# A state-space layer's decay product, made whole or in two halves of a block's tokens

## The chip, the cores and the metric

One core of one Trainium2 chip runs the whole program. The time is the device time of one execution in microseconds (us). A profile gives, for one execution, the start and length of every instruction on the core's engines: TensorE (PE, with its weight loads listed apart as PEld), VectorE (DVE), ScalarE (ACT), GpSimd (POOL) and SyncE (SP), which here issues the transfers.

## The reference

A trunk of two layers over 256 tokens of width 2048. The first layer is a Mamba-2 mixer (SSD): a projection to z, x, B, C and dt, a causal convolution, a state-space scan, a gate and a grouped RMS norm, and a projection back. The second is a dilated attention with shared keys and values. Both are followed by a residual and a LayerNorm. The part that matters here is the scan, cut from the reference; the sequence is one chunk of 256 tokens, so the state that comes in is zero and y is y_diag:

```python
G, K, P, N = 8, 8, 64, 128        # groups, heads per group, head width, state
acum  = jnp.cumsum(ac, axis=1)                        # log decays, per token and head
seg   = acum[:, :, None] - acum[:, None, :]           # from token s to token l
decay = jnp.exp(jnp.where(causal, seg, -jnp.inf))
cb    = jnp.einsum("blgn,bsgn->blsg", cc, bc)         # C_l . B_s, per group
y_diag = jnp.einsum("blsgk,bsgkp->blgkp", cb[..., None] * decay, xc)
...
y = y + (xs * D_skip[:, None]).reshape(bsz, L, SSD_D_INNER)
y = y * jax.nn.silu(z)
```

For each of 64 heads this is the product of a lower triangular matrix of 256 x 256 (C.B times the decay) with the head's 256 x 64 columns of x times dt.

## The kernel before

All large products are made with weights split into two rounded parts (`hi` and `lo`, lines 92 to 98), in three matmuls for each pair of tiles: lines 121 to 123 (channels in the partitions), 169 to 171 (tokens in the partitions), and 145 and 148 in the second layer. Their weights are streamed from memory in pieces of 512 KB (line 89), split by ScalarE (line 95) and VectorE (line 97). These products fill nearly all of TensorE's time from the first layer to the end.

The scan runs group by group, eight heads in each. Each group has three stages:

- `stage1(g)` (line 548) makes C.B for three blocks of 128 x 128 tokens (lines 554 and 555; source and target both in the first 128 tokens, both in the second, and from the first to the second), the two diagonal blocks of the decay of every head on ScalarE (lines 567 and 569), their product `seg` (line 570), and by transposes (line 578) the columns `xd`, which are x times dt.
- `stage2(g)` (line 595) makes the part that comes from the first block to the second (line 600, one product for all eight heads of the group, the decay being split off), and then, for each of the two blocks `b` of 128 tokens, eight products into one PSUM tile `py` of 128 x 512: one for each head, with the head's 128 x 128 matrix `seg` as stationary operand and its 64 columns of `xd` as moving operand (line 608). VectorE adds `py` to y (line 609) and multiplies by the gate (line 610); ScalarE squares it and sums (line 611).
- `stage3(g)` (line 616) applies the norm's factor.

All operands of line 608 are f32; the profile records each such product as two passes, that is two weight loads and two matmuls.

The order of the work is that of the program's lines as the framework's scheduler places them on each engine: between `stage1(g)` and `stage2(g)` stands the projection `product("z", g + 1)`, so that TensorE has products of the next group while ScalarE makes the decays. TensorE executes in the placed order. Around line 608's blocks stand line 600 ahead and the projections' products (lines 121 to 123 and 169 to 171) behind; the last group's blocks are interleaved with the last projection's products. Two more lines appear in the prediction for their shapes: 461, transposes of dt with 64 rows in use, and 544 and 258, transposes with 64 and 16 columns.

The PSUM tiles `py` come from the pool `aux2`, with two buffers, so the next block's products don't wait for VectorE to have read the last one.

Of the kernel before, what the change touches and what calls it, by code (L numbers as in the profile page):

```python
# [49 lines left out]
def trunk(ctx, tc, xT, x, c, par, cst, bias, lnrow, ada, wdt, win, wout, wk, wv, wbin, wbout, out):  # L50
    nc = tc.nc
    V, S, T, PO = nc.vector, nc.scalar, nc.tensor, nc.gpsimd
# [148 lines left out]
    def rsqrt(v, tag):  # L201

        y = sm.tile(list(v.shape), F32, name=tag + "y")
        sh = sm.tile(list(v.shape), I32, name=tag + "s")
        V.tensor_scalar(sh, v.bitcast(I32), 1, None, op0=ALU.logical_shift_right)
        V.tensor_tensor(y.bitcast(I32), magic[:, :v.shape[1]], sh, op=ALU.subtract)
        t = sm.tile(list(v.shape), F32, name=tag + "t")
        for _ in range(3):
            V.tensor_tensor(t, y, y, op=ALU.mult)
            V.scalar_tensor_tensor(t, t, -0.5, v, op0=ALU.mult, op1=ALU.mult)  # L210
            V.scalar_tensor_tensor(y, t, 1.5, y, op0=ALU.add, op1=ALU.mult)
        return y
# [73 lines left out]
    with ExitStack() as cA:  # L286
# [14 lines left out]
        with ExitStack() as cS:  # L301
# [293 lines left out]
            def stage2(g, segs, xd, cb, xo):  # L595

                ss = sm.tile([P, 2], F32, name="ss")

                po = aux.tile([P, 512], F32, name="aux")
                T.matmul(po, cb[:, 2, :], xo, start=True, stop=True)  # L600
                V.tensor_tensor(xo.rearrange("p (h e) -> p h e", h=HPG), po.rearrange("p (h e) -> p h e", h=HPG),
                                dec[:, 1, g * HPG:(g + 1) * HPG, None].to_broadcast([P, HPG, 64]), op=ALU.mult)
                V.tensor_tensor(y[g][:, 1, :], xo, y[g][:, 1, :], op=ALU.add)
                for b in range(2):
                    py = aux2.tile([P, 512], F32, name="py")
                    for hh in range(HPG):
                        e_ = slice(64 * hh, 64 * hh + 64)
                        T.matmul(py[:, e_], segs[hh // 4][:, hh % 4, b, :], xd[:, b, e_], start=True, stop=True)  # L608
                    V.tensor_tensor(y[g][:, b, :], py, y[g][:, b, :], op=ALU.add)
                    V.tensor_tensor(y[g][:, b, :], y[g][:, b, :], sz[g][:, b, :], op=ALU.mult)  # L610
                    S.activation(py, y[g][:, b, :], AF.Square, accum_out=ss[:, b:b + 1])
                ms = sm.tile([P, 2], F32, name="ms")
                V.tensor_scalar(ms, ss, 1.0 / 512, EPS, op0=ALU.mult, op1=ALU.add)
                return rsqrt(ms, "a")
# [8 lines left out]
            for g in range(G - 1):  # L623
                if g == 1:
                    pin[0] = latest[-1].ins
                    queue(wp1, [(0, "gate", kt) for kt in range(KT)])
                    jobs.append(lambda: gate_out(0))
                if g % 2 == 1:
                    product("bc", g + 1)
                product("xs", g + 1)  # L630
                if rs is not None:
                    stage3(g - 1, rs)
                st1 = stage1(g)
                if g < G - 2:
                    product("z", g + 1)
                rs = stage2(g, *st1)
# [7 lines left out]
            product("z", G - 1, last_scores)  # L644
            drain()
            stage3(G - 1, stage2(G - 1, *st1))
        aux = ctx.enter_context(tc.tile_pool(name="auxb", bufs=2, space=PSUM, reuse_waits="tile"))

# [428 lines left out]
```

## Time and profile before

| | |
|---|---|
| median of 3 runs | 1275.34 us (1275.26 to 1276.29) |
| span of the profiled execution, first to last instruction | 1272.5 us |
| median less that span (the profiled execution's own whole time isn't listed apart) | 2.8 us |
| instructions | 19056 |
| TensorE busy, matmuls / weight loads | 1236.6 us / 1078.7 us |
| VectorE / ScalarE busy | 1034.5 us / 704.0 us |
| read from memory | 332.47 MB, 263 GB/s over the span |

A line of a group of instructions reads: source line, engine, operation, written tile <- read tiles, for TensorE the rows*columns of the array that it uses, shape out, count | busy us in all, ns of one | idle time of the engine just before them, and what ended it. A line of the timeline reads: start, length, engine, source line, operation, and xN where N like it follow one another. Matmuls are pipelined: their records overlap, so the distance from one to the next, not the length of one, is what a pass takes. In the chain, each piece is the time that counts towards the end.

### The profile page before, as it was taken

How to read it: one execution, taken by the hardware profiler on the slowest of the kernel's cores; microseconds unless marked ns; L12 is line 12 of the kernel's file. 1: busy time of each engine (PE TensorE's matmuls, PEld its weight loads, DVE VectorE, ACT ScalarE, POOL GpSimd, SP SyncE). 2: the span in 40 equal slices, each digit the busy share in tenths (PEclk: the TensorE clock that was granted, in tenths of full speed). 3: DMA queues.
4: the chain of work that ended last, by engine and by line, in shares of the span. 5: the costliest groups of instructions: out<-in, count | busy, mean ns of one | idle time of the engine just before them, and what ended most of it. 6: DMA issues, size and time to landing. Idle time of an engine off the chain costs nothing.

```text
span 1272.5 us, 19056 instructions
## 1 busy us (share of the span) xinstructions
PE 1236.6 (97%) x7222; PEld 1078.7 (85%) x7222; DVE 1034.5 (81%) x1498; ACT 704.0 (55%) x1035; POOL 0.2 (0%) x4
## 2 busy tenths in 40 slices
PE   4999999999999999999999999999999999999997
PEld 4889989899898999778888788888878888888885
DVE  6999986999998878869776678878888867758876
ACT  3655577757677777764344445434345645444731
POOL 0000000000000000000000000000000000000000
PEclk9999999999999999999999999999999999999999
DMA  9999968696866546468988469989998774463751
GB/s 386 423 420 422 420 211 298 224 341 234 314 247 208 157 149 216 167 216 292 338 282 282 160 195 353 357 328 348 357 381 316 235 240 130 127 204 100 222 192 66
DMA packets 80588, 335.89 MB, mean 264 GB/s; under 512 B 9105, under 2 KB 9329, under 8 KB 67697
## 3 DMA queue, kind: packets, MB, share of 16 engines
q1 hardware_dynamic: 80496, 334.69, 73.5%
q8 instruction: 56, 0.92, 0.3%
q14 instruction: 36, 0.29, 0.1%
HBM read 332.47 MB, written 2.18 MB: 263 GB/s over the span
## 4 chain that ended last, share of the span: by engine, by line
PE 85%; DVE 8%; DMA 3%; issue 2%; ACT 1%; SPq 0%; DVEq 0%; ACTq 0%
PE acc L145 14%; PE acc L171 12%; PE acc L170 12%; PE acc L169 12%; PE acc L148 7%; PE acc L123 7%; PE acc L121 7%; PE acc L122 7%; DVE araw L247 2%; DVE wlo L97 2%; PE py L608 2%; PE aux L850 1%; DMA araw<-in_ada 1%; DMA raw<-in_wk 1%; PE po L873 1%
## 5 line engine op out<-in xcount | busy, mean ns | idle before, releaser
L95 ACT ACTIVATE whi<-raw 128x1024 fp32r<-128x1024 f32 x392 | 411.3, 1058 | 369.4 <-PE acc L171 127.3
L97 DVE TENSOR_TENSOR wlo<-raw,whi 128x1024 fp32r<-128x1024 f32 x392 | 473.3, 1220 | 140.3 <-ACT whi L95 139.5
L145 PE MATMUL acc<-actT,whi 128*128 128x512 f32 x896 | 285.9, 398 | 0.0
L170 PE MATMUL acc<-wlo,actT 128*128 128x512 f32 x688 | 269.7, 392 | 1.1 <-DVE wlo L97 0.9
L169 PE MATMUL acc<-whi,actT 128*128 128x512 f32 x688 | 266.7, 394 | 0.9 <-ACT actT L663 0.9
L121 PE MATMUL acc<-actT,whi 128*128 128x256 f32 x768 | 217.4, 285 | 17.5 <-ACT actT L398 17.3
L247 DVE SCALAR_TENSOR_TENSOR araw<-araw,cb__72 128x2048 f32<-128x2048 f32 x96 | 219.2, 2284 | 14.6 <-DMA araw<-in_ada 14.5
L123 PE MATMUL acc<-actT,wlo 128*128 128x256 f32 x768 | 214.9, 285 | 4.9 <-DVE wlo L97 4.9
L122 PE MATMUL acc<-actT,whi 128*128 128x256 f32 x768 | 217.1, 284 | 0.0
L148 PEld LDWEIGHTS acc<-actT,wlo 128*128 128x128 f32 x896 | 167.0, 188 | 42.1 <-DVE wlo L97 5.0
L148 PE MATMUL acc<-actT,wlo 128*128 128x256 f32 x896 | 180.9, 282 | 1.9 <-DVE wlo L97 1.2
L171 PE MATMUL acc<-whi,actT 128*128 128x512 f32 x432 | 168.7, 391 | 0.0
L121 PEld LDWEIGHTS acc<-actT,whi 128*128 128x128 f32 x768 | 147.7, 193 | 18.7 <-ACT actT L398 17.5
L170 PEld LDWEIGHTS acc<-wlo,actT 128*128 128x128 f32 x688 | 129.3, 188 | 29.1 <-DVE wlo L97 3.4
L123 PEld LDWEIGHTS acc<-actT,wlo 128*128 128x128 f32 x768 | 146.5, 193 | 6.0 <-DVE wlo L97 5.8
L169 PEld LDWEIGHTS acc<-whi,actT 128*128 128x128 f32 x688 | 128.7, 188 | 26.7 <-ACT actT L663 1.4
L122 PEld LDWEIGHTS acc<-actT,whi 128*128 128x128 f32 x768 | 148.1, 193 | 0.3
L145 PEld LDWEIGHTS acc<-actT,whi 128*128 128x128 f32 x896 | 137.5, 189 | 0.3
L171 PE MATMUL acc<-whi,ylo 128*128 128x512 f32 x256 | 100.5, 393 | 0.0
L171 PEld LDWEIGHTS acc<-whi,actT 128*128 128x128 f32 x432 | 81.1, 188 | 16.6
L171 PEld LDWEIGHTS acc<-whi,ylo 128*128 128x128 f32 x256 | 48.0, 188 | 9.7
L319 DVE SCALAR_TENSOR_TENSOR cacc<-acc,prm,cacc 128x253 f32<-128x253 f32 (+2 forms) x96 | 42.1, 474 | 6.1 <-ACT cacc L316 5.8
(251 smaller groups left out, 1110.2 us busy)
## 6 DMA issues: line engine op xcount, KB each, us to landing
araw<-in_ada SPq DMA_DIRECT2D x96, 1024.0 KB, 7.5
raw<-in_win SPq DMA_DIRECT2D x160, 512.0 KB, 5.6
raw<-in_wout SPq DMA_DIRECT2D x64, 512.0 KB, 4.8
raw<-in_wbin SPq DMA_DIRECT2D x64, 512.0 KB, 4.3
raw<-in_wv SPq DMA_DIRECT2D x48, 512.0 KB, 5.4
raw<-in_wk SPq DMA_DIRECT2D x48, 512.0 KB, 7.7
cbc<-cumd SPq DMA_DIRECT2D x16, 512.0 KB, 5.2
raw<-in_wbout SPq DMA_DIRECT2D x16, 512.0 KB, 4.7
```

Source lines behind the costliest of these rows:

```text
L95: copied.append(S.activation(hi, raw, AF.Copy))
L97: latest.append(V.tensor_tensor(lo, raw, hi.bitcast(F32), op=ALU.subtract))
L121: T.matmul(o, hi[:, k, c_], ahi[:, kt, :], start=first, stop=False, skip_group_check=True)
L122: T.matmul(o, hi[:, k, c_], alo[:, kt, :], start=False, stop=False, skip_group_check=True)
L123: T.matmul(o, lo[:, k, c_], ahi[:, kt, :], start=False, stop=kt == k1 - 1, skip_group_check=True)
L145: T.matmul(ps[n], hi[:, k, n * P:n * P + P], xp[:, kt], start=kt == 0, stop=False, skip_group_check=True)
L148: T.matmul(ps[n][:, 0, :], lo[:, k, n * P:n * P + P], xhi[:, kt, :], start=False, stop=kt == KT - 1, skip_group_check=True)
L169: T.matmul(o, h_, hi[:, k, :], start=kt == k0, stop=False, skip_group_check=part)
L170: T.matmul(o, h_, lo[:, k, :], start=False, stop=False, skip_group_check=part)
L171: end = T.matmul(o, l_, hi[:, k, :], start=False, stop=kt == k1 - 1, skip_group_check=part)
L247: V.scalar_tensor_tensor(raw, raw, 1.0, cb_, op0=ALU.mult, op1=ALU.mult, accum_out=mod[layer][:, ct, j:j + 1])
L319: V.scalar_tensor_tensor(acc[:, o:], ps[:, :L - o], w[:, j:j + 1], acc[:, o:], op0=ALU.mult, op1=ALU.add)
```

## The change

Each head's product with a block's 128 tokens is issued as two: one with the first 64 columns of the stationary matrix, which are the first 64 of the block's tokens, into partitions 0 to 63 of `py`, and one with the other 64 columns into partitions 64 to 127. Both read the same 64 moving columns. The sum over the 128 source tokens, the results and what follows stay as they are.

```diff
                     for hh in range(HPG):
                         e_ = slice(64 * hh, 64 * hh + 64)
-                        T.matmul(py[:, e_], segs[hh // 4][:, hh % 4, b, :], xd[:, b, e_], start=True, stop=True)
+                        for t_ in (slice(0, 64), slice(64, 128)):
+                            T.matmul(py[t_, e_], segs[hh // 4][:, hh % 4, b, t_], xd[:, b, e_], start=True, stop=True)
                     V.tensor_tensor(y[g][:, b, :], py, y[g][:, b, :], op=ALU.add)
```

## The prediction

> **What bounds the kernel now.** I read the page's busy times and its chain first, then the chain in order of time for the places where the changed line stands, then that line's own groups, and last the timeline of TensorE (PE) and of its weight loads (PEld) around one of its blocks.
>
> ```profile
> PE 1236.6 (97%) x7222; PEld 1078.7 (85%) x7222; DVE 1034.5 (81%) x1498; ACT 704.0 (55%) x1035; POOL 0.2 (0%) x4
> ...
> PE 85%; DVE 8%; DMA 3%; issue 2%; ACT 1%; SPq 0%; DVEq 0%; ACTq 0%
> ```
>
> TensorE is busy for 97% of the span and carries 85% of the chain that ends last. In the stage that the change touches it is no different; the row below is that of the 310 us in which all products of line 608 lie. Its first numbers are the length of the stretch and PE's busy time.
>
> ```profile
> 225.00:535.00 310.00, 306.22 (x2154) 284.12 (x2152) 278.56 (x449) 228.54 (x375) 0.00 (x0) 1.00 0.65 225
> ```
>
> PE leaves 3.8 us of 310 idle, at a granted clock of 1.00. So what PE needs more or less for line 608 is nearly all time of the kernel, as far as those products are on the chain. Which are, the chain in order of time tells (start, length, what):
>
> ```profile
> 229.24 1.73 PE py L608 x16
> ...
> 232.00 1.73 PE py L608 x16
> ...
> 287.85 3.52 PE py L608 x32
> ...
> 338.63 3.52 PE py L608 x32
> ...
> 382.63 3.52 PE py L608 x32
> ...
> 429.36 3.52 PE py L608 x32
> ...
> 502.48 3.52 PE py L608 x32
> ...
> 525.16 0.61 PE py L608 x6
> 533.58 1.08 PE py L608 x10
> ```
>
> The line's source view says how many there are in all, and the timeline of PE shows the three runs that the chain lacks:
>
> ```profile
> L608 PEld LDWEIGHTS py<-xd,seg x256: 186/192/192, 228.9 to 534.3; 128*128 128x128 f32 x128
> L608 PE MATMUL py<-xd,seg x256: 217/275/275, 229.1 to 534.4; 128*128 128x64 f32 x128
> ```
>
> ```profile
> 472.36 3.68 PE L608 MATMUL py<-xd,seg 128*128 128x64 f32 x32
> ...
> 518.43 1.02 PE L608 MATMUL py<-xd,seg 128*128 128x64 f32 x8
> ...
> 520.71 1.00 PE L608 MATMUL py<-xd,seg 128*128 128x64 f32 x8
> ```
>
> Each of the 128 f32 products is recorded as two passes, each a weight load and a matmul: 256 passes. They lie in 12 unbroken runs. Nine of these, with 16+16+5x32+6+10 = 208 passes (0.81 of all), are on the chain; at 472 and 518 VectorE is later, and PE has some time to spare.
>
> **What one pass costs, and what sets it.** The weight loads of one run, then the matmuls:
>
> ```profile
> 287.26 0.19 PEld L608 LDWEIGHTS py<-xd,seg 128*128 128x128 f32 x1 [0.24 <-issue]
> 287.69 3.54 PEld L608 LDWEIGHTS py<-xd,seg 128*128 128x128 f32 x31 [0.24 <-issue]
> ```
>
> ```profile
> 286.83 1.02 PE L600 MATMUL aux<-xo,cb 128*128 128x512 f32 x2
> 287.69 3.68 PE L608 MATMUL py<-xd,seg 128*128 128x64 f32 x32
> ```
>
> ```profile
> L600 PE MATMUL aux<-xo,cb 128*128 128x512 f32 x16 | 8.2, 594 | 0.0
> ```
>
> 31 loads of 0.192 us start within 3.54 us, so they follow each other by (3.54 - 0.19)/30 = 111.6 ns. The moving side would be quicker: the two passes of L600 are 1.02 - 0.59 = 0.43 us apart (0.59 is the mean of one, by its row of the groups) for 512 columns, 0.84 ns a column, or 54 ns for 64 columns. So a pass of line 608 is bound by loading 128 stationary columns, not by streaming 64. All of it now: 256 x 111.6 ns = 28.6 us.
>
> **The change part by part.** It makes 256 products of 64 stationary columns out of 128 of 128 columns, so 512 passes. Operands, values, the sums into py, the waits of line 609 on it, and every DMA stay; no step is moved and no wait is added. Only PE gets 256 more loads and 256 more matmuls.
>
> *A load of 64 columns.* No row has a plain f32 load of 64 columns. Other groups show how a load shrinks with its columns:
>
> ```profile
> L608 PEld LDWEIGHTS py<-xd,seg 128*128 128x128 f32 x256 | 30.4, 192 | 4.3 <-issue 3.3 <-DVE xd L580 0.5 <-DVE s L583 0.2
> L578 PEld LDWEIGHTS aux<-cc,xs 128*128 128x128 f32 x64 | 7.5, 141 | 1.7 <-DVE cb L557 1.1
> L544 PEld LDWEIGHTS aux<-cc,cumT 128*64 128x64 f32 x2 | 0.2, 110 | 0.2
> ...
> L258 PEld LDWEIGHTS aux<-cc,mod 128*16 128x16 f32 x2 | 0.2, 93 | 0.0
> ```
>
> The last three are transposes, which load faster: 141, 110 and 93 ns for 128, 64 and 16 columns, about 0.4 ns a column over a fixed 87 ns. Line 608's plain load takes 192, so (192 - 87)/128 = 0.82 ns a column: 105 ns of the 111.6 are columns and 6.6 are overhead. With 64 columns I estimate 52.5 + 6.6 = 59 ns a pass, just above the 54 ns of streaming. 512 x 59 = 30.2 us against 28.6: **+1.6 us**. The nearest row from above is line 461, the only one with 64 moving columns and a load of about this streaming length (transposes of a 64-row tile):
>
> ```profile
> 173.40 0.19 PEld L169 LDWEIGHTS acc<-whi,actT 128*128 128x128 f32 x1
> 173.94 0.20 PEld L461 LDWEIGHTS acc<-cc,dtrow 64*128 64x128 f32 x2 [0.35 <-ACT dtrow L458]
> 174.21 0.19 PEld L170 LDWEIGHTS acc<-wlo,actT 128*128 128x128 f32 x1
> ```
>
> ```profile
> 173.39 0.39 PE L171 MATMUL acc<-whi,actT 128*128 128x512 f32 x1
> 173.62 0.39 PE L169 MATMUL acc<-whi,actT 128*128 128x512 f32 x1
> 173.94 0.34 PE L461 MATMUL acc<-cc,dtrow 64*128 64x64 f32 x2
> 174.21 0.50 PE L170 MATMUL acc<-wlo,actT 128*128 128x512 f32 x1
> ```
>
> Its two loads (141 ns each, from its neighbour L578) span 0.20 us, so they are 0.06 us apart. At 63 ns the term is 512 x 63 - 28.6 = +3.7 us; at the streaming bound of 54 ns, -1.0 us. I take 59, whose slope comes from the load itself.
>
> *Going into and out of halves of the array.* The same rows price a change of tile. Elsewhere a load starts with the matmul ahead of it (173.40 and 173.39). Behind line 461's 64-row tile it doesn't: the second matmul started at about 173.94 + 0.34 - 0.22 = 174.06 (0.22 being the shortest matmul of 64 columns in line 608's row), and the next load, full size, only at 174.21: **0.15 us** later than in the usual order, and the matmul with it. The entry can't be read there, since that load waited for ScalarE (0.35 us). Behind line 258, which has only 16 columns but all rows, there is no such gap, the load comes with the matmul:
>
> ```profile
> 973.10 0.09 PEld L258 LDWEIGHTS aux<-cc,mod 128*16 128x16 f32 x1
> 973.32 0.30 PEld L169 LDWEIGHTS acc<-whi,actT 128*128 128x128 f32 x2
> ```
>
> ```profile
> 973.32 0.27 PE L258 MATMUL aux<-cc,mod 128*16 128x128 f32 x1
> 973.35 0.71 PE L169 MATMUL acc<-whi,actT 128*128 128x512 f32 x2
> ```
>
> So a switch costs between nothing and 0.15 us. I take 0.15, and as much for an entry, since the change, unlike line 258, places products in a part of the array that doesn't begin at its edge (PSUM's partitions from 64 on). 12 runs, 2 x 0.15 each: +3.6 us; for the nine runs on the chain 2.7.
>
> The Trainium skill, "TensorEngine Tiling (Array Packing)", section "Tiling Modes", says that changing the tiling mode, as opposed to the tile, drains TensorE. By it entry and exit both cost, and the two halves inside a run, being of one mode, don't: that is the 3.6 us; by the row alone, which shows an exit, it would be 1.8 us. The row agrees with the rule as far as it goes, for a 64-row tile and not for a 64-column one.
>
> *Sum.* On the chain: 0.81 x 1.6 + 2.7 = 1.3 + 2.7 = **+4.0 us**; with nothing absorbed at 472 and 518, +5.2. The span is 1272.5 us; the runs' median is 1275.34, 2.8 us around it, which I leave as it is: 1275.3 + 4.0 = **1279.3 us**. Behind py nothing else gets late first: in PE's order the products of the next group's columns follow, which have their weights, and the VectorE sum of line 609 starts later by what a run got longer, up to 0.1 + 0.15 us.
>
> **The rivals.**
>
> *The two halves load side by side (faster).* If a load into the second half of the array runs while the first half still loads, two passes take the time of one: 256 x 59 = 15.1 us, -13.5 us on the columns, +3.6 on switches: -9.9 if all of it counts, 0.81 x -13.5 + 2.7 = -8.2 on the chain: 1265.4 to **1267.1 us**. It decides from 28.6 - 3.6 = 25.0 us for 512 passes, under 49 ns each. Against it: in the rows above a load starts no earlier than the matmul ahead of it (287.26 is the start of L600's second pass, 286.83 + 0.43), and the change issues two passes into the same half in a row. For it: no product of this trace alternates between two halves, so no row excludes it. The Trainium skill's same section states that tiles operate independently and that different tiles can execute loads and matmuls in parallel; by that rule the time is this rival's. Chance 0.27.
>
> *Passes can't follow each other faster than about 110 ns (much slower).* No run of more than two passes in this trace is quicker than line 608's or the transposes' (about 109 ns). If instruction supply, or a load that can't hide beside a matmul in a half array (53 + 54 + 6 ns), holds a pass at 107 to 113 ns, or a 64-column load takes as long as a whole one, the columns cost 512 x 107 to 113 - 28.6 = 26 to 29 us; the spare time at 472 and 518 is used up by that, and with the switches it is +30 to +33: **1305 to 1308 us**. Against it: line 461's two passes in 0.06 us, and loads that shrink with their columns. Chance 0.15.
>
> *More switches (slower).* In the last group the runs have 8, 8, 6 and 10 passes, with other products between them. If the order written for twice as many instructions breaks all eight groups so, that is 32 runs, 64 x 0.15 = 9.6 us, and with 1.6 **1286.5 us**. Chance 0.06.
>
> *Nothing to see.* Switches in the column direction are free, as behind L258: 1.3 us are left, **1276.6 us**. Chance 0.10. That the change doesn't do what it says can't be: the halves are written out as py's and seg's slices.
>
> **How the numbers follow.** The forecast has 0.42, with a range of its own from 1278 (cheaper entries) to 1285 us (63 ns a pass and all switches, +7.3, plus a few more breaks). A measurement of this kernel tells 0.2% from no change, 2.6 us. Faster by more: 0.27. Within: 0.10. Slower by more: 0.42 + 0.15 + 0.06 = 0.63. The range takes in the faster rival and the broken order, from 1265 to 1290 us; it leaves out the 110 ns rival (0.15) and a little below.
>
> **What would show it.** Line 608's groups should have 512 loads of about 139 ns and 512 matmuls, of form 128*64. A run of 64 passes should be about 3.8 us long instead of 3.6, with loads 59 ns apart; the first load of a run, and the first behind it, should start about 0.15 us after the matmul ahead of it would let it. Loads of both halves at one time, or a run of 64 under 3.1 us, would prove me wrong on the faster side; a run of 7 us on the slower. The other lines should keep their means, and the chain its shares.

## The result, and the profile after

The changed kernel takes 1267.27 us (median of 5 runs, 1265.41 to 1268.09) against 1276.29 us for the kernel before, run beside it (5 runs, 1275.26 to 1276.87). The ratio is 0.9928, 95% interval 0.9917 to 0.9938: 9.2 us less, between 7.9 and 10.6. In a later set of runs, on chip 9, the ratio was 0.9942 (0.9927 to 0.9956). Ratios and intervals are worked out from all runs, so they aren't the quotients of the medians; the two differ by up to 0.0015, 2 us. The forecast was +4.0; the rival in which the two halves load side by side had given -8.2 to -9.9.

The page of the changed kernel, busy times and chain; the lines below the change have moved down by one, so the product is now line 609.

```profile
PE 1227.3 (97%) x7478; PEld 1065.9 (84%) x7478; DVE 1033.1 (82%) x1498; ACT 704.7 (56%) x1035; POOL 0.2 (0%) x4
...
PE 80%; DVE 10%; DMA 5%; ACT 2%; issue 2%; SPq 0%; DVEq 0%; ACTq 0%
```

PE has 256 passes more and is busy for 9.3 us less; its share of the chain has gone from 85% to 80%, and VectorE (8% to 10%) and transfers (3% to 5%) take more of it. The source view of the line, then the timeline of the weight loads around the run that was shown of the kernel before:

```profile
L609 PEld LDWEIGHTS py<-xd,seg x512: 132/138/139, 229.6 to 526.5; 128*64 128x64 f32 x171
L609 PE MATMUL py<-xd,seg x512: 221/222/271, 229.7 to 526.6; 128*64 128x64 f32 x171
```

```profile
287.04 0.19 PEld L600 LDWEIGHTS aux<-xo,cb 128*128 128x128 f32 x1
287.98 1.95 PEld L609 LDWEIGHTS py<-xd,seg 128*64 128x64 f32 x64 [0.76 <-issue]
290.00 0.19 PEld L121 LDWEIGHTS acc<-actT,whi 128*128 128x128 f32 x1
```

The same stretch for the matmuls:

```profile
287.04 1.02 PE L600 MATMUL aux<-xo,cb 128*128 128x512 f32 x2
287.98 2.08 PE L609 MATMUL py<-xd,seg 128*64 128x64 f32 x64
290.00 0.39 PE L121 MATMUL acc<-actT,whi 128*128 128x256 f32 x1
```

A load is 138 ns long, but 64 of them start within 1.95 - 0.14 = 1.81 us, 28.7 ns apart. A narrower window of the loads' timeline shows how:

```profile
287.98 0.20 PEld L609 LDWEIGHTS py<-xd,seg 128*64 128x64 f32 x4 [0.76 <-issue]
```

Four loads begin within 0.20 - 0.14 = 0.06 us: two nearly together, and two more half a tenth of a microsecond later. The matmuls overlap in the same way: 64 of them start within 2.08 - 0.22 = 1.86 us, 29.5 ns apart. Below, a pass in two halves is put at 29.2 ns, between the two.

In the kernel before, the run at 287.69 was followed by the first row below; the second row is the next product of the same shape here:

```profile
291.18 0.36 PE L121 MATMUL acc<-actT,whi 128*128 128x256 f32 x1
```

```profile
290.22 0.28 PE L122 MATMUL acc<-actT,whi 128*128 128x256 f32 x1
```

From the start of L600 to the place where L121 really streams (its record is 0.39 long here and 0.36 before, where such records take 0.28, so it is taken to have waited for 0.11 and 0.08 us) it is 290.11 - 287.04 = 3.07 us, and it was 291.26 - 286.83 = 4.43: 1.36 us less in a run of a whole group. Eight groups give 10.9 us. The first and the last group still have six runs between them in place of two, four more pairs of mode changes, 4 x 0.29 = 1.2 us back: -9.7 us on PE's work. The stage's row shows what was given up again:

```profile
225.00:527.00 302.00, 297.20 (x2411) 270.99 (x2410) 277.43 (x449) 228.35 (x376) 0.00 (x0) 1.00 0.66 230
```

PE is idle for 4.8 us of the stage, where it was 3.8: about -8.7 remains. The two profiles' spans differ by 1272.5 - 1263.6 = 8.9 us. The last product came 7.8 us earlier, the end 8.9 us. The 1.1 us between them come from the transposes right behind (line 661, 662 after): they begin 7.8 us earlier and end 8.9 us earlier, at 572.7 us in place of 581.6, with 2.9 us of waiting for `ylo` in place of 4.5. Why they waited less isn't shown.

### The profile page after: what moved, and what is told of

The parts are those of the page before. It is cut to its first block, busy times and chain, and to the rows that moved or that the text cites. A ratio compares the mean times of both kernels' runs of the same rounds, so it can differ in the third digit from the quotient of the medians.

```text
span 1263.6 us, 19569 instructions
## 1 busy us (share of the span) xinstructions
PE 1227.3 (97%) x7478; PEld 1065.9 (84%) x7478; DVE 1033.1 (82%) x1498; ACT 704.7 (56%) x1035; POOL 0.2 (0%) x4
## 4 chain that ended last, share of the span: by engine, by line
PE 80%; DVE 10%; DMA 5%; ACT 2%; issue 2%; SPq 0%; DVEq 0%; ACTq 0%
PE acc L145 13%; PE acc L171 12%; PE acc L170 12%; PE acc L169 12%; PE acc L148 7%; PE acc L123 6%; PE acc L121 6%; PE acc L122 6%; DMA raw<-in_wk 3%; DVE wlo L97 2%; DVE araw L247 2%; DMA araw<-in_ada 2%; DVE cacc L319 1%; PE aux L851 1%; PE po L874 1%
## 5 line engine op out<-in xcount | busy, mean ns | idle before, releaser
L121 PE MATMUL acc<-actT,whi 128*128 128x256 f32 x768 | 217.8, 286 | 17.4 <-ACT actT L398 17.3
L121 PEld LDWEIGHTS acc<-actT,whi 128*128 128x128 f32 x768 | 147.9, 193 | 19.1 <-ACT actT L398 17.5
```

Of the source, the lines that this page charges most:

```text
L121: T.matmul(o, hi[:, k, c_], ahi[:, kt, :], start=first, stop=False, skip_group_check=True)
```

## The experiments

**Theory A**: two parts of the array, each with its own 64 columns, work side by side. Within one part a pass follows the last by about 58 ns, as forecast; the gain comes from overlap between parts. **Rival B**: a pass with 64 columns is simply that short, wherever it lies. **Rival C**: 29 ns is a least distance of instructions. A fourth reading is that the framework's other order of the remaining work made the gain. All ratios below are to the kernel before, run on the same chip.

### Half by half

```diff
-for hh in range(HPG):
-    for t_ in (slice(0, 64), slice(64, 128)):
+for t_ in (slice(0, 64), slice(64, 128)):
+    for hh in range(HPG):
```

> Same 256 products of 64 stationary columns, but in each block the eight heads' first halves come first and then the eight second halves, so the half of the array changes once a block and not with every product. Theory A (the two halves of the array work side by side, a pass in one half takes 58 ns, and only products that alternate between halves can overlap): 16 passes in a row in one half, so 58 ns a pass, 64 x 58 = 3.7 us a run of 64 passes and not 2.1; 512 x 58 = 29.7 us against 28.6 before, with the switches +4 to +5 us: about 1280 us. Rival B (a pass with 64 columns simply takes 29 ns, the halves don't matter, or the two passes of one product overlap): a run of 64 stays at 2.1 us and the time at 1267.

Measured: 1276.13 us, ratio 0.9997 (0.9983 to 1.0011), between 2.2 us less and 1.4 more. The timeline of its matmuls, a whole run, and then the beginning of it:

```profile
290.85 3.41 PE L609 MATMUL py<-xd,seg 128*64 128x64 f32 x64
```

```profile
290.85 0.62 PE L609 MATMUL py<-xd,seg 128*64 128x64 f32 x7
```

Seven passes in one half: the first record is 0.27 long, so by their ends they are (0.62 - 0.27)/6 = 58 ns apart, with the same instructions that take 29 in the change. Rival B falls, and so does its second form, since the two passes of one product follow each other here too. The run is shorter than 63 x 58.3 ns = 3.67 us, since at each of its three changes of half some passes of the second half begin beside the last of the first. With that, PE's columns are 8 x (3.41 - 0.22) = 25.5 us and change by -3.1, the switches by +3.6: +0.5, inside the interval. The +4 to +5 that I had expected left this look-ahead out.

### Turns after two and after four heads

```diff
-for hh in range(HPG):
-    for t_ in (slice(0, 64), slice(64, 128)):
+for h0, t_ in ((h0, t_) for h0 in range(0, HPG, 2) for t_ in (slice(0, 64), slice(64, 128))):
+    for hh in range(h0, h0 + 2):
```

> The halves take turns after every two heads (4 passes in one half, then 4 in the other). In the half-by-half kernel a run of 64 passes with 3 changes of half had matmuls over 3.19 us, 0.48 less than 63 x 58.3 ns: each change of half won 0.16 us, about three passes, which began beside the last ones of the other half. Theory A with such a look-ahead of about three passes: 15 changes of half in a run would win 2.4 us, more than side by side can give, so nearly full overlap, a run of 1.9 to 2.1 us, and the time of the change within 2 us. If the overlap needs products that alternate one by one: a run of over 2.5 us and 5 us more than the change.

and with 4 in place of 2:

> Turns after four heads (8 passes): 7 changes of half in a run of 64 passes, 7 x 0.16 = 1.1 us won of 3.67: a run of about 2.55 us between its first and last matmul, 0.7 us longer than with turns at every head, 8 runs: about 5 us more than the change, so 4 us less than before. If the time does not go by the overlap in the runs but by the framework's order, no such step between this one, the two-head turns and the change.

Measured, on one chip with the change itself:

> The change itself again, beside the three others on one chip: 0.9928 of before, 9 us less, as measured.

| turn after | time, us | ratio (interval) | matmuls of a run, first to last start |
|---|---|---|---|
| one head (the change) | 1268.58 | 0.9942 (0.9927 to 0.9956) | 1.86 us |
| two heads | 1267.22 | 0.9933 (0.9918 to 0.9948) | 1.91 us |
| four heads | 1269.94 | 0.9953 (0.9936 to 0.9969) | 2.47 us |
| eight heads (half by half, other chip) | 1276.13 | 0.9997 (0.9983 to 1.0011) | 3.19 us |

The last column is from such rows of the timelines, the length less the 0.22 us of one matmul; two heads, then four:

```profile
289.13 2.13 PE L609 MATMUL py<-xd,seg 128*64 128x64 f32 x64
```

```profile
289.57 2.69 PE L609 MATMUL py<-xd,seg 128*64 128x64 f32 x64
```

Both runs are as long as expected (1.9 to 2.1, about 2.55). The same 256 products take between 1.9 and 3.2 us a run by nothing but the order of the halves. The kernel's time goes with it at the wide end, from half by half to the rest; between one, two and four heads, where 8 x 0.6 = 5 us lie at most, the intervals overlap, and four heads lost less than its runs did (-6.0 us, -8.2 to -4.0, where -4 was expected).

Part of the scatter is the granted clock. Its mean over a run was 0.995 to 0.998 in the four runs of the change here, with a span of 1267.7 us at 0.995 and of 1264.5 at 0.998, and 0.998 or 0.999 in those with turns after two heads. As an estimate, each span times its clock, less the same of the kernel before, gives -10.5, -9.0, -6.8 and -1.6 us for one, two, four and eight heads, which is the order of the runs' lengths; two heads aren't shown to be quicker than one. The fourth reading, the framework's order, isn't excluded for a microsecond or two, since no run held that order fixed. It isn't needed for the gain: the runs' own shortening gives -9.7 us, and with the same number of products half by half wins next to nothing.

### Quarters

```diff
-for t_ in (slice(0, 64), slice(64, 128)):
+for t_ in (slice(32 * i, 32 * i + 32) for i in range(4)):
```

> 512 products of 32 stationary columns, one for each quarter of a block's tokens: 1024 passes. Theory A with streaming as the limit: a pass streams 64 columns in 54 ns whatever its stationary width, four quarters side by side give one pass for each 14.6 ns, a head takes the same 117 ns as in halves: about 1267 us. Rival C (29 ns is the least distance of two passes, for instance from instruction supply, and not a property of two halves): 1024 x 29.2 = 29.9 us, 15 us more than halves: about 1282 us. Weight loads alone (half as many columns, four at a time) would give half of it, 7.5 us less than halves: about 1260 us.

Measured: 1272.44 us, ratio 0.9972 (0.9963 to 0.9982), 3.6 us less than before. One run of its matmuls:

```profile
291.39 1.99 PE L609 MATMUL py<-xd,seg 128*32 128x64 f32 x128
```

128 passes start within 1.99 - 0.22 = 1.77 us, 14 ns apart, so 29 ns was no least distance, and rival C falls. Four passes take 56 ns: that is close to the streaming of 64 columns, forecast at 54, and half as many stationary columns did not shorten it. A run is about as long as in halves, yet the time is 4 to 6 us longer than the change's (-3.6 against -7.4 and -9.2, not on one chip), where the same was expected. Some of that is seen. Its timeline has 16 runs where the change has 12, 8 x 0.15 = 1.2 us of switches, and PE waits longer for VectorE's weight splits, as the waits of PE in the stage show, quarters first and then the change (total, times, longest, us):

```profile
PE acc L123 <- DVE wlo L97: 5.8, 5, 2.2
```

```profile
PE acc L123 <- DVE wlo L97: 3.4, 2, 2.1
```

That is 2.4 us more. The rest, up to 2 us, stays open; the order in which the framework placed the other work differs between the two, and no run held it fixed.

### Every other head in halves

```diff
-for t_ in (slice(0, 64), slice(64, 128)):
+for t_ in (slice(0, 64), slice(64, 128)) if hh % 2 else (slice(0, 128),):
```

> Odd heads in two halves as in the change, even heads whole as before, alternating: 8 changes of mode in a block, 128 in all, where the change has 24. Columns: 128 whole passes x 111.6 ns + 256 half passes x 29.2 = 14.3 + 7.5 = 21.8 us, 6.8 less than before. Theory A with 0.15 us for each change of mode: 128 x 0.15 = 19.2 us, together +12.4: about 1288 us. If a change of mode costs nothing: -6.8, 1269 us. If it only costs when 512-column products stand beside it (a drain of about 0.1 us less): 128 x 0.05 = 6.4, so no difference from before, 1276 us.

Measured: 1289.97 us, ratio 1.0121 (1.0094 to 1.0148), +15.4 us (12.0 to 18.9). A run of 16 heads, from its first matmul to L121 behind it:

```profile
289.81 5.01 PE L609 MATMUL py<-xd,seg 128*128 128x64 f32 x48
294.75 0.39 PE L121 MATMUL acc<-actT,whi 128*128 128x256 f32 x1
```

To the place where L121 streams it is 294.75 + 0.11 - 289.81 = 5.05 us. 16 whole passes and 32 half ones would be 16 x 111.6 + 32 x 29.2 ns = 2.72 us; the other 2.33 us are 16 changes of mode, 0.146 us each. So the price that line 461 showed for a 64-row tile holds for 64-column ones, as a mean of going into and out of the mode. It rests on this run and not on the whole time: the medians differ by 13.5 us, and the four runs had mean granted clocks of 0.990 to 0.997, where those of the kernel before had 0.996 to 1.000; at 0.990 and 0.991 the spans were 1292.6 and 1290.5 us, at 0.997 they were 1283.0 and 1285.7. So some of the 15.4 us is the clock.

### The moving side in two

```diff
-    e_ = slice(64 * hh, 64 * hh + 64)
-    for t_ in (slice(0, 64), slice(64, 128)):
-        T.matmul(py[t_, e_], segs[hh // 4][:, hh % 4, b, t_], xd[:, b, e_], start=True, stop=True)
+    for e_ in (slice(64 * hh, 64 * hh + 32), slice(64 * hh + 32, 64 * hh + 64)):
+        T.matmul(py[:, e_], segs[hh // 4][:, hh % 4, b, :], xd[:, b, e_], start=True, stop=True)
```

> Also 256 products in place of 128, but each with the whole 128-column stationary matrix and 32 of the head's 64 moving columns; one tile, no change of mode. It has the change's number of instructions. If loads of 128 columns set the time at 111.6 ns a pass, as read before: 512 x 111.6 = 57.1 us, +28.5: about 1305 us. If the change's gain came from the order that the framework chose for twice as many products, and not from the array's halves, part of it shows here: under 1297 us.

Measured: 1329.32 us, ratio 1.0412 (1.0390 to 1.0435), +53 us, nearly twice what was expected. Twice the products do not gain anything by themselves. The first part and the rest of one run of 64 passes show what the expectation lacked; then windows of these two parts, of the second part of another run, and of the whole stage, where the number after POOL's is the granted clock:

```profile
293.25 5.35 PE L608 MATMUL py<-xd,seg 128*128 128x32 f32 x47
```

```profile
298.42 3.82 PE L608 MATMUL py<-xd,seg 128*128 128x32 f32 x17
```

```profile
293.25:298.42 5.17, 5.17 (x49) 5.16 (x47) 3.66 (x9) 2.06 (x4) 0.00 (x0) 1.00 0.02 7
298.42:302.05 3.63, 3.63 (x20) 3.63 (x19) 1.40 (x4) 2.93 (x9) 0.00 (x0) 0.50 0.00 0
...
506.68:514.15 7.47, 7.47 (x38) 7.47 (x37) 1.89 (x3) 3.19 (x10) 0.00 (x0) 0.50 0.00 0
...
215.00:600.00 385.00, 381.85 (x2554) 354.97 (x2553) 299.65 (x490) 250.61 (x411) 0.00 (x0) 0.94 0.59 202
```

At a clock of 1.00, 47 passes are (5.35 - 0.28)/46 = 110 ns apart (0.28 is the median length of a matmul of the line). With 32 moving columns a pass takes as long as with 64, so the load of 128 columns sets it, as read before. Then the clock falls to 0.50, and the 17 that are left are (3.82 - 0.40)/16 = 214 ns apart (0.40 is the longest). In the run that starts at 503.50 it falls after about 3 us. Over the stage the clock is 0.94, which costs 385 x 0.06 = 23 us, as an estimate for a stage in which PE is nearly always busy; with the 28.5 expected that is 51.5, and the spans differ by 1323.1 - 1272.5 = 50.6 us.

### Line 600 in halves too

```diff
-T.matmul(po, cb[:, 2, :], xo, start=True, stop=True)
+for t_ in (slice(0, 64), slice(64, 128)):
+    T.matmul(po[t_, :], cb[:, 2, t_], xo, start=True, stop=True)
```

> The change, and line 600's product (512 moving columns, 430 ns a pass, set by streaming) also in two halves. Theory A: two halves side by side stream for as long as the whole did, 2 passes x 430 ns, so no gain from its columns; in group 0 and in the last group line 600 no longer parts two runs, up to 4 changes of mode or 0.6 us less: the time of the change within 1 us. If halves make any product faster: 8 x 0.43 = 3.4 us less than the change. If the second half's streaming waits for the first's: 8 x 0.86 = 6.9 us more.

Measured: 1268.37 us, ratio 0.9941 (0.9926 to 0.9955), where the change beside it had 0.9942. Its matmuls of line 600 (601 there):

```profile
289.28 1.08 PE L601 MATMUL aux<-xo,cb 128*64 128x512 f32 x4
```

Four passes in 1.08 us where two whole ones took 1.02: side by side, and no shorter, as expected where streaming 512 columns sets the time. The kernel's time is the change's, as expected too. None of these versions is shown to beat the change.

## Why the prediction was wrong

**What bounds the kernel, and what sets a pass.** Right. Line 608 was bound by loading 128 columns: half the moving columns left a pass at 110 ns. Line 600, bound by streaming, gained nothing from halves.

**The price of a load and of a pass in one half.** Right: 139 ns and 59 ns were forecast, 138 and 58 measured (half by half). How much of the 58 is loading isn't shown: in a quarter, with half the columns to load, a pass still takes 56, so streaming alone may nearly set it. Line 461's own loads are 138 ns by its source view, and not 141 as taken from its neighbour; its 0.06 us stay.

**The changes of mode.** Right: 0.15 us forecast, 0.146 measured as a mean over entry and exit. In the change's own run the passes alone would have saved 32 x 111.6 - 64 x 29.2 ns = 1.70 us; it saved 1.36, which leaves 0.17 us for each of its two changes. Both ways have a share: the first product comes 0.94 us after the start of L600 in place of 0.86, and behind the run the last matmul starts at 287.98 + 2.08 - 0.22 = 289.84 and the next load only at 290.00. The Trainium skill, "TensorEngine Tiling (Array Packing)", section "Tiling Modes", has a drain at a change of mode and not at a change of tile; the runs agree, with 0.15 us between modes and passes of two halves 29 ns apart.

**The step that failed** is the multiplication: 512 x 59 ns = 30.2 us, +1.6 us. It added the passes up one behind the other. I had argued that a load starts no earlier than the matmul ahead of it, from rows in which no two products in a row used different columns of the array, and carried that over to products in two parts of it; to their overlap I gave only 0.27. In two halves, 512 passes take 512 x 29.2 = 15.0 us, -13.6 instead of +1.6. With +3.6 for the switches that is -10.0, against -9.2 (-10.6 to -7.9) and, in the later set, -7.4 (-9.3 to -5.6).

**The second argument against the overlap**, that two passes into the same half come in a row, was wrong as well: turns after two heads, four passes in a row, overlap almost fully. The matmuls of the second half begin beside the last ones of the first.

**The range**, 1265 to 1290 us, holds the result only because it had been stretched to take in the rival; the forecast, 1279.3, and the larger chance, 0.63, lay on the other side. The rival's own working held, both its columns (-13.5) and its point of decision, 49 ns a pass: the measured 29 lies well below. Of the share on the chain (0.81), the comparison of the two stages suggests that nearly all of the saving counted, with 1 us given back to waits on VectorE.

The Trainium skill, "TensorEngine Tiling (Array Packing)", section "Tiling Modes", states that different tiles can load and multiply in parallel; the runs agree, 29.2 ns a pass in two halves against 58 in one. The Trainium skill, "TensorE: Matmul & The Clock Gate", section "Part 3: Packing small matmuls — row/col tiling", states that a load overlaps matmuls in flight only where the row group differs; here both halves use all 128 rows, and the loads of line 609 start 28.7 ns apart while matmuls with records of 222 ns are in flight. The ends of those records are modelled; as far as they tell, the measurement decides against that sentence for column halves.

## What to carry to other kernels

Ask of a small product whether its pass is set by loading the stationary columns or by streaming the moving ones: in the profile, the distance of its loads against the distance of a wide product's passes, scaled to its columns. Where loading sets it, as in line 608, splitting the stationary columns over parts of the array and alternating between them lets the parts work side by side, until streaming is the limit; where streaming sets it, as in line 600, nothing was won. A forecast then takes the passes of one part alone, not the sum over the parts, and adds the switches. Keep such products in long unbroken runs, since each change of mode costs 0.15 us here, which is as much as five half passes.

## What was not expected of the hardware

A price read for one tile can't be added up over two: a pass took 58 ns in one half alone, 29 with two halves in turn, and 14 with four quarters in turn. And in each of the six runs of 56 or 64 passes with 32 moving columns under 128-column loads, the granted clock fell from 1.00 to 0.50 between 3 and 6 us after the run's start, though PE was never idle in it; a pass then took 214 ns in place of 110. The kernel before, with 64 moving columns and runs of 3.5 us at most, kept 1.00, and so did the first such run of 32 passes (3.5 us, at 231.07). Whether the fewer columns or the longer run does it was not separated.
